# Mixture-of-experts kernel on one Trainium2 core: gathered rows scaled on the ScalarE and plainly transposed, routing by 8 one-hot products of nine columns

## Chip, core and metric

The kernel runs as one program on one core of a Trainium2 chip. The metric is the device time of one execution in microseconds (us); lower is better. The engines are named as the profile names them: PE (TensorE, matmuls), PEld (its weight loads), DVE (VectorE), ACT (ScalarE), POOL (GpSimd) and SP (SyncE, here the queue that issues the weight loads from memory).

## What is computed

One layer of a diffusion backbone over 1024 latent tokens of width 1024: a token mixer (differential attention and a short convolution), then an expert-choice mixture of experts with 16 experts of 128 token slots each. The change lies in the mixture of experts:

```python
logits = jnp.einsum('btd,de->bte', x_tok, w_router)
aff = jax.nn.softmax(logits, axis=-1)
g, idx = lax.top_k(jnp.swapaxes(aff, 1, 2), cap)      # cap = 128
xs = jax.vmap(lambda xt, ix: xt[ix])(x_tok, idx)
hg = jnp.einsum('becd,edf->becf', xs, w_gate)
hu = jnp.einsum('becd,edf->becf', xs, w_up)
y = jnp.einsum('becf,efd->becd', jax.nn.silu(hg) * hu, w_down) * g[..., None]
out = zeros.at[idx].add(y)
```

where `x_tok` is the normalised and modulated stream: each token's row times its reciprocal root mean square (one number per token), then a scale and a shift per channel.

## The kernel before

The mixer takes the first part of the span. From about 717 us on a loop runs over the 16 experts, called e0 to e15 here. An expert has 6 chunks of weights, and a chunk has 4 tiles q0 to q3 of 128 x 1024 f32 numbers (`raw`, 512 KB), which the SP queue loads ahead into 30 buffers. Chunks c0 and c2 are the two halves of the gate projection (products into `hg`), c1 and c3 those of the up-projection (`hu`), c4 and c5 the down-projection (`pyy`, two banks).

Every f32 product is made from three reduced ones. `split` (lines 155 to 159) divides a tile: ACT writes the rounded upper part `whi` (L157), then DVE the rest `wlo` (L158). There are 4 buffers of each (`NSP`), so the upper part of a tile can be written once PE is through with the tile four before. `mm3` then issues L162, L163 and L164: upper by upper, `wlo` by upper, `whi` by the lower part of the other operand. A tile takes 6 matmuls, a chunk 24, an expert 144.

For each expert `route` finds its tokens: DVE compares positions into a one-hot tile `oh` (L1460), 24 small products of 3 columns (L1465) sum token number (three parts), gate and token scale into the bank `pi`, ACT turns the first column into the index `idx` (L1467), POOL gathers the 128 rows `xs` from memory (L1469), DVE copies the three sums to `slot` (L1472) and builds `dgx`, the identity times the token scale (L1474). `xsplit` then transposes and scales at once, as eight f32 matmuls of `xs` blocks with `dgx` (L1511) into two banks `ptt`; ACT applies scale and shift per channel (`xsy`, L1513, eight instructions) and `split` gives `xsh` and `xsl`.

The loop body in code order: c0 products; the routing of the next expert (`nxt = route(e + 1)`); c1 products, `glu`; c2 products; transposes of the first activation half (`tsplit`, four, L1481, giving `ach` and `acl`); c3 products, `glu`; `xsplit` of the next expert; c4 and c5 with the transposes of the second half after the first tile (`TSJ`); then ACT scales the result by the gate (`y`, L1604) and POOL adds the rows into memory (`ffS`, L1605). e15 is different: its last chunks aren't split.

The code order isn't the queue order. SP's queue is written by hand; those of PE, DVE, ACT and POOL are laid out in this part by the framework when the program is built, by its own estimate of when operands are ready, and each engine then runs its own queue strictly in that order. So a change in one instruction can move others.

Of the kernel before, what the change touches and what calls it, by code (L numbers as in the profile page):

```python
# [10 lines left out]
F32 = mybir.dt.float32  # L11
# [3 lines left out]
AF = mybir.ActivationFunctionType  # L15
OP = mybir.AluOpType
AX = mybir.AxisListType
# [3 lines left out]
P = 128  # L21
# [5 lines left out]
E = 16  # L27
KT = 8
# [119 lines left out]
def build(tc, nc, I, out, dbg=None):  # L148
    V, S, G, PE, SY = nc.vector, nc.scalar, nc.gpsimd, nc.tensor, nc.sync
# [17 lines left out]
    with es:  # L167
# [4 lines left out]
        sm = es.enter_context(tc.tile_pool(name="sm", bufs=4))  # L172
        dr = es.enter_context(tc.tile_pool(name="dr", bufs=1, space=DRAM))
        pgA = es.enter_context(tc.tile_pool(name="pgA", bufs=NPA))
# [5 lines left out]
        def page(p, name, dt=F32, shape=(P, D)):  # L180
            return p.tile(list(shape), dt, name=name, tag="pg")

        def bank(shape, name):
            return psB.tile(list(shape), F32, name=name, tag="b")
# [219 lines left out]
        for i, o in enumerate(ORDER.split()):  # L404
            if i == NL0:
                npm = const("npm", [P, KT])
                ident = const("ident", [P, P])
# [100 lines left out]
        for i in range(10):  # L508
# [6 lines left out]
            for j in range(2):  # L515
                S.dma_start(out=vS[:, :, j, i, :].rearrange("h p e -> p h e"),
                            in_=f(hl[:, j, :]).rearrange("p (h e) -> p h e", h=H))
# [727 lines left out]
        for i, (h, qt) in enumerate(seq):  # L1245
            j = i + 2
# [26 lines left out]
            c = None  # L1273
            if SO[i // 16] == 0:
                if j < N:
                    c = score()
                x0 = transp(cs[i], qt, 0)
                x1 = transp(cs[i], qt, 1)
# [179 lines left out]
        def route(e):  # L1458
            oh = x1.tile([P, KT, P], BF, name="oh")
            V.tensor_tensor(out=oh, in0=late["iota"][:, None, :].to_broadcast([P, KT, P]),  # L1460
                            in1=pos[:, :, e:e + 1].to_broadcast([P, KT, P]), op=OP.is_equal)
            pi = bank([P, 3], "pi")
            for j in range(KT):
                for k in range(3):
                    PE.matmul(pi, oh[:, j, :], tokb[:, j, e, k, :], start=(j + k == 0), stop=(j == KT - 1 and k == 2))  # L1465
            idx = sm.tile([P, 1], I32, name="idx")
            S.activation(idx, pi[:, 0:1], AF.Copy)  # L1467
            xs = x1.tile([P, D], F32, name="xs")
            G.indirect_dma_start(out=xs, out_offset=None, in_=hS[:, :],  # L1469
                                 in_offset=bass.IndirectOffsetOnAxis(ap=idx[:, :1], axis=0))  # L1470
            s = sm.tile([P, 3], F32, name="slot")
            V.tensor_copy(out=s, in_=pi)  # L1472
            dg = x1.tile([P, P], F32, name="dgx")
            V.tensor_scalar(dg, ident, s[:, 2:3], None, op0=OP.mult)  # L1474
            g = s[:, 1:2]
            return idx, g, xs, s, dg

        def tsplit(src, k0, hi, lo):
            pp = bank([P, 4, P], "ptt")
# [21 lines left out]
                hi, lo = w[kt // 2]  # L1501
                mm3(ps, xh_[:, kt, :], xl_[:, kt, :], hi[:, kt % 2, :], lo[:, kt % 2, :], kt == 0, kt == KT - 1)

        def xsplit(xs, dg, eng=V):

            hi, lo = x1.tile([P, KT, P], F32R, name="xsh"), x1.tile([P, KT, P], F32R, name="xsl")
            for k in range(0, KT, 4):
                pp = bank([P, 4, P], "ptt")
                y = x1.tile([P, 4, P], F32, name="xsy", bufs=2)
                for j in range(4):  # L1510
                    PE.matmul(pp[:, j, :], xs[:, (k + j) * P:(k + j + 1) * P], dg, start=True, stop=True)  # L1511
                for j in range(4):
                    S.activation(y[:, j, :], pp[:, j, :], AF.Identity, bias=mv[:, 1, k + j:k + j + 1],  # L1513
                                 scale=mv[:, 2, k + j:k + j + 1])
                split(hi[:, k:k + 4, :], lo[:, k:k + 4, :], y, eng)
            return hi, lo
# [27 lines left out]

        cur = route(0)
        first = chunk(0, 0)
        xh_, xl_ = xsplit(cur[2], cur[4], V)
        eD.close()
        e5.close()
        for e in range(E):  # L1550
# [23 lines left out]
                prod(hu, xh_, xl_, chunk(e, 2 * fh + 1))  # L1574
                acts.append(glu(hg, hu))
            if e + 1 < E:
                xh_, xl_ = xsplit(nxt[2], nxt[4])
            pys = [eacc("pyy") for _ in range(2)]
            if e + 1 == E:

# [53 lines left out]
```

## Time and profile before

| | us |
|---|---|
| Median of 3 runs (1338.62 to 1341.94) | 1339.59 |
| The profiled execution's own time | 1337.48 |
| Its span in the profile | 1335.7 |
| PE busy | 1233.5 (92%) |
| DVE busy | 1076.9 (81%) |
| ACT busy | 794.9 (60%) |
| POOL busy | 67.9 (5%) |

Shares are means over the whole span. In the expert loop they differ: the slices from 780 us to 1180 us show PE at 9 tenths or more, DVE and ACT at 8 to 9, and the granted PE clock at full speed.

### The profile page before, as it was taken

To read this page: it belongs to the slowest core of one execution; us is meant where nothing else is said; L and a number is where in the kernel's file an instruction comes from. 1 tells how busy PE (TensorE), PEld (TensorE's weight loads), DVE (VectorE), ACT (ScalarE), POOL (GpSimd) and SP (SyncE) were. 2 spreads that over 40 slices of the span, in tenths; PEclk is the share of its full clock that TensorE was granted. 3 is DMA by queue.
4 is the path that set the end of the run, shared out by engine and by line. 5 is a ranking of instruction groups with operands and counts; after the bars stand their busy time and mean duration, and the time that the engine had idled before them with its cause. 6 is when DMAs were issued, how large, how long until landed. Compare 5 with 4: busy or idle time off the path is not lost. (4 is left out here: it accounts for less than half of the span.)

```text
span 1335.7 us, 18448 instructions
## 1 busy us (share of the span) xinstructions
PE 1233.5 (92%) x6407; PEld 1005.1 (75%) x6407; DVE 1076.9 (81%) x1834; ACT 794.9 (60%) x1183; POOL 67.9 (5%) x64
## 2 busy tenths in 40 slices
PE   6999999999999799989945999999999999999993
PEld 2587887888888578767844888888888888877761
DVE  5972565979698867798967999999999999888865
ACT  5731112434344544455443988888888888887861
POOL 0000000000000000000000000000000000010022
PEclk8999999999999899999956999999999999999997
DMA  9449448455466974333297999999999999999497
GB/s 350 140 81 319 148 148 252 135 166 182 134 179 183 297 192 143 129 120 124 107 407 244 320 393 370 384 381 380 372 378 373 377 377 371 379 356 363 120 377 161
DMA packets 139053, 347.69 MB, mean 260 GB/s; under 512 B 16976, under 2 KB 59472, under 8 KB 138320
## 3 DMA queue, kind: packets, MB, share of 16 engines
q1 hardware_dynamic: 109760, 306.14, 64.7%
q0 software_dynamic: 7056, 25.69, 7.3%
q10 hardware_dynamic: 22144, 14.68, 3.9%
q8 instruction: 50, 0.82, 0.2%
q14 instruction: 43, 0.35, 0.1%
HBM read 297.17 MB, written 49.30 MB: 259 GB/s over the span
## 5 line engine op out<-in xcount | busy, mean ns | idle before, releaser
L158 DVE TENSOR_TENSOR wlo<-raw,whi 128x1024 fp32r<-128x1024 f32 x376 | 440.8, 1220 | 33.1 <-ACT whi L157 27.9
L157 ACT ACTIVATE whi<-raw 128x1024 fp32r<-128x1024 f32 x376 | 388.7, 1066 | 61.7 <-PE hu L164 28.3
L1131 ACT ACTIVATE e<-ps,nm 128x1280 f32<-128x1280 f32 x64 | 84.4, 1327 | 65.5 <-DVE nm L1127 65.3
L1127 DVE TENSOR_REDUCE nm<-ps 128x1 f32<-128x1280 f32 x64 | 92.8, 1484 | 14.5 <-PE ps L1118 14.3
L162 PE MATMUL hu<-whi,xsh 128*128 128x512 f32 x256 | 102.7, 401 | 1.6 <-ACT whi L157 1.6
L163 PE MATMUL hu<-wlo,xsh 128*128 128x512 f32 x256 | 101.8, 398 | 0.8 <-DVE wlo L158 0.8
L164 PE MATMUL hg<-whi,xsl 128*128 128x512 f32 x256 | 99.8, 390 | 1.0 <-DVE xsl L158 1.0
L163 PE MATMUL hg<-wlo,xsh 128*128 128x512 f32 x256 | 100.4, 392 | 0.0
L164 PE MATMUL hu<-whi,xsl 128*128 128x512 f32 x256 | 100.4, 392 | 0.0
L162 PE MATMUL hg<-whi,xsh 128*128 128x512 f32 x256 | 100.0, 391 | 0.0
L1118 PE MATMUL ps<-KK,q 128*128 128x512 f32 (+1 forms) x384 | 90.8, 383 | 8.8 <-ACT e L1131 6.5
L1163 ACT ACTIVATE ath<-ptr 128x512 fp32r<-128x512 f32 (+1 forms) x96 | 47.8, 525 | 85.5 <-PE ptr L1158 85.1
L163 PE MATMUL pyy<-wlo,ach 128*128 128x512 f32 x240 | 95.0, 396 | 1.4 <-DVE wlo L158 0.9
L162 PE MATMUL pyy<-whi,ach 128*128 128x512 f32 x240 | 94.0, 402 | 0.0
L164 PE MATMUL pyy<-whi,acl 128*128 128x512 f32 x240 | 93.8, 391 | 0.0
L1118 PEld LDWEIGHTS ps<-KK,q 128*128 128x128 f32 x384 | 65.2, 202 | 20.9 <-ACT e L1131 9.1
L671 PE MATMUL pf<-xh,wh 128*128 128x512 f32 x192 | 75.1, 391 | 0.9 <-DVE gc L689 0.9
L675 PE MATMUL pf<-xh,wl 128*128 128x512 f32 x192 | 75.8, 395 | 0.0
L673 PE MATMUL pf<-xl,wh 128*128 128x512 f32 x192 | 75.2, 392 | 0.0
L1166 DVE TENSOR_TENSOR atl<-ptr,ath 128x512 fp32r<-128x512 f32 (+1 forms) x96 | 55.5, 596 | 14.3 <-ACT ath L1163 14.1
L162 PEld LDWEIGHTS hu<-whi,xsh 128*128 128x128 f32 x256 | 48.3, 189 | 11.4 <-ACT whi L157 2.1
L163 PEld LDWEIGHTS hu<-wlo,xsh 128*128 128x128 f32 x256 | 48.5, 190 | 11.1 <-DVE wlo L158 1.8
(316 smaller groups left out, 2649.1 us busy)
## 6 DMA issues: line engine op xcount, KB each, us to landing
raw<-in_we SPq DMA_DIRECT2D x384, 512.0 KB, 9.4
wa<-in_wa SPq DMA_DIRECT2D x32, 512.0 KB, 7.5
wraw<-in_wF SPq DMA_DIRECT2D x20, 512.0 KB, 5.2
waw<-in_wa SPq DMA_DIRECT2D x16, 512.0 KB, 6.9
q<-qS SPq DMA_DIRECT2D x64, 128.0 KB, 4.4
mS<-hl SPq DMA_DIRECT2D x48, 128.0 KB, 5.3
vS<-hv ACTq DMA_DIRECT2D x20, 256.0 KB, 6.0
KK<-kS SPq DMA_DIRECT2D x16, 320.0 KB, 8.5
```

What stands on the lines that cost most here:

```text
L157: i = S.activation(hi, src, AF.Copy)
L158: eng.tensor_sub(lo, src, f(hi))
L162: PE.matmul(ps, wh, mh, start=first, stop=False)
L163: PE.matmul(ps, wh, ml, start=False, stop=False)
L164: PE.matmul(ps, wl, mh, start=False, stop=last)
L671: PE.matmul(ps, wh[:, kt, :], xh[kt][:, sl], start=first, stop=False)
L673: PE.matmul(ps, wh[:, kt, :], xl[kt][:, sl], start=False, stop=False)
L675: PE.matmul(ps, wl[:, kt, :], xh[kt][:, sl], start=False, stop=last)
L1118: PE.matmul(ps[:, m, k0:k0 + n], q[:, m, j, :], KK[:, m, k0:k0 + n], start=(j == 0), stop=(j == 1))
L1127: V.tensor_reduce(out=c[1][-1], in_=c[0][:, m, :], axis=AX.X, op=OP.max, negate=True)
L1131: S.activation(e, c[0][:, m, :], AF.Exp, bias=c[1][3 + m], accum_out=l[:, m:m + 1])
L1166: V.tensor_sub(x[1], x[2], f(x[0]))
```

## The change

The eight products with `dgx` become plain transposes with the identity. The token scale is applied before them, by one ACT instruction over the gathered rows (in place; for e15 into a page of its own, because the unscaled rows are added at the end). For all but e0 this instruction must queue behind the last `whi` of chunk c3. The 24 products of 3 columns become 8 of 9 columns, and DVE sums the three parts (`tensor_reduce`) and makes the index (`tensor_copy`).

```diff
-            pi = bank([P, 3], "pi")
+            pi = bank([P, 9], "pi")
             for j in range(KT):
-                for k in range(3):
-                    PE.matmul(pi, oh[:, j, :], tokb[:, j, e, k, :], start=(j + k == 0), stop=(j == KT - 1 and k == 2))
+                PE.matmul(pi, oh[:, j, :], tokb[:, j, e, :, :].rearrange("p k c -> p (k c)"), start=(j == 0),
+                          stop=(j == KT - 1))
+            s = sm.tile([P, 3], F32, name="slot")
+            V.tensor_reduce(out=s, in_=pi.rearrange("p (k c) -> p c k", c=3), axis=AX.X, op=OP.add)
             idx = sm.tile([P, 1], I32, name="idx")
-            S.activation(idx, pi[:, 0:1], AF.Copy)
+            V.tensor_copy(out=idx, in_=s[:, 0:1])
             xs = x1.tile([P, D], F32, name="xs")
             G.indirect_dma_start(out=xs, out_offset=None, in_=hS[:, :],
                                  in_offset=bass.IndirectOffsetOnAxis(ap=idx[:, :1], axis=0))
-            s = sm.tile([P, 3], F32, name="slot")
-            V.tensor_copy(out=s, in_=pi)
-            dg = x1.tile([P, P], F32, name="dgx")
-            V.tensor_scalar(dg, ident, s[:, 2:3], None, op0=OP.mult)
-            g = s[:, 1:2]
-            return idx, g, xs, s, dg
+
+            xn = xs if e + 1 < E else page(pgA, "xn")
+            return idx, s[:, 1:2], xs, s, xn
...
-        def xsplit(xs, dg, eng=V):
+        def xsplit(cur, eng=V, behind=None):
 
             hi, lo = x1.tile([P, KT, P], F32R, name="xsh"), x1.tile([P, KT, P], F32R, name="xsl")
+            xs = cur[4]
+            if behind is None:
+                S.activation(xs, cur[2], AF.Copy, scale=cur[3][:, 2:3])
+            else:
+                with tc.issue_after(behind.ins):
+                    S.activation(xs, cur[2], AF.Copy, scale=cur[3][:, 2:3])
             for k in range(0, KT, 4):
                 pp = bank([P, 4, P], "ptt")
                 y = x1.tile([P, 4, P], F32, name="xsy", bufs=2)
                 for j in range(4):
-                    PE.matmul(pp[:, j, :], xs[:, (k + j) * P:(k + j + 1) * P], dg, start=True, stop=True)
+                    PE.transpose(out=pp[:, j, :], in_=xs[:, (k + j) * P:(k + j + 1) * P], identity=ident)
...
-        xh_, xl_ = xsplit(cur[2], cur[4], V)
+        xh_, xl_ = xsplit(cur, V)
...
             if e + 1 < E:
-                xh_, xl_ = xsplit(nxt[2], nxt[4])
+                xh_, xl_ = xsplit(nxt, behind=lasts[0])
```

The queues come out differently at three places. First ACT in e1 to e8, around the end of c2, before:

```order
L157 ACTIVATE whi<-raw 128x1024 x5
L1467 ACTIVATE idx<-pi 128x1
L1541 ACTIVATE act<-hg 128x512
L157 ACTIVATE whi<-raw 128x1024 x8
L157 ACTIVATE ach<-ptt 128x512
L1541 ACTIVATE act<-hg 128x512
L157 ACTIVATE whi<-raw 128x1024 x4
L1513 ACTIVATE xsy<-ptt,mv 128x128 x5
```

and with the change:

```order
L157 ACTIVATE whi<-raw 128x1024 x5
L1546 ACTIVATE act<-hg 128x512
L157 ACTIVATE whi<-raw 128x1024 x8
L157 ACTIVATE ach<-ptt 128x512
L1546 ACTIVATE act<-hg 128x512
L1511 ACTIVATE xs<-xs,slot 128x1024
L157 ACTIVATE whi<-raw 128x1024 x4
L1518 ACTIVATE xsy<-ptt,mv 128x128 x5
```

The index has gone, and the scale of `xs` stands ahead of the four splits of c4. On PE the `pi` products have moved at the same time from between c0 and c1 of an expert to inside the down-projection of the expert before (in e0 to e8 behind two matmuls of c5's first tile, in e9 to e13 behind c4's second tile).

Second, ACT in e10, from the end of c2 to the end of the transposed rows, with the change:

```order
L1546 ACTIVATE act<-hg 128x512
L157 ACTIVATE ach<-ptt 128x512
L157 ACTIVATE whi<-raw 128x1024 x2
L1511 ACTIVATE xs<-xs,slot 128x1024
L157 ACTIVATE whi<-raw 128x1024 x2
L1518 ACTIVATE xsy<-ptt,mv 128x128 x5
L157 ACTIVATE xsh<-xsy 128x512
L1518 ACTIVATE xsy<-ptt,mv 128x128 x3
L157 ACTIVATE whi<-raw 128x1024
L157 ACTIVATE xsh<-xsy 128x512
L157 ACTIVATE whi<-raw 128x1024
L157 ACTIVATE ach<-ptt 128x512
```

Here only c4's q0 and q1 are split ahead of the `xsy` instructions; q2 and q3 stand behind them. This layout holds in e9 to e13; before the change its like stands in e12 to e14 only. In e14 of the changed kernel all four tiles of c4 stand behind the `xsy` instructions.

Third, DVE in e10 from the end of c3 on, before:

```order
L1542 TENSOR_TENSOR act<-act,hu 128x512
L158 TENSOR_TENSOR wlo<-raw,whi 128x1024
L158 TENSOR_TENSOR xsl<-xsy,xsh 128x512
L158 TENSOR_TENSOR acl<-ptt,ach 128x512
L158 TENSOR_TENSOR xsl<-xsy,xsh 128x512
L158 TENSOR_TENSOR wlo<-raw,whi 128x1024 x11
L1460 TENSOR_TENSOR oh<-iota,pos 128x1024
```

and with the change:

```order
L1547 TENSOR_TENSOR act<-act,hu 128x512
L158 TENSOR_TENSOR wlo<-raw,whi 128x1024
L158 TENSOR_TENSOR xsl<-xsy,xsh 128x512
L1467 TENSOR_REDUCE slot<-pi 128x3
L1460 TENSOR_TENSOR oh<-iota,pos 128x1024
L158 TENSOR_TENSOR xsl<-xsy,xsh 128x512
L158 TENSOR_TENSOR wlo<-raw,whi 128x1024 x2
L158 TENSOR_TENSOR acl<-ptt,ach 128x512
L158 TENSOR_TENSOR wlo<-raw,whi 128x1024 x7
L1469 CAST idx<-slot 128x1
```

The sum of the routing products and the next one-hot tile now stand ahead of the second `xsl` and of the `wlo` of c4's q2 and q3.

## Rows read from the trace of the kernel before

**Rows 1.** Windows: us; busy us (xinstructions) of PE, PEld, DVE, ACT, POOL; clock; DMA; GB/s.

```profile
1086.00:1122.00 36.00, 36.00 (x193) 29.91 (x193) 32.96 (x34) 31.44 (x42) 3.22 (x2) 1.00 1.01 375
```

**Rows 2.** Timeline of PE in e2 (start us, us, engine line op, count).

```profile
802.45 0.76 PE L1465 MATMUL pi<-tokb,oh 128*128 128x3 bf16 x24
803.07 0.48 PE L162 MATMUL hu<-whi,xsh 128*128 128x512 f32 x1
...
820.02 1.95 PE L1511 MATMUL ptt<-dgx,xs 128*128 128x128 f32 x16
821.72 0.48 PE L162 MATMUL pyy<-whi,ach 128*128 128x512 f32 x1
...
827.95 0.41 PE L163 MATMUL pyy<-wlo,ach 128*128 128x512 f32 x1
...
833.21 0.39 PE L162 MATMUL hg<-whi,xsh 128*128 128x512 f32 x1
```

**Rows 3.** Timeline of ACT in the same expert.

```profile
816.20 1.06 ACT L157 ACTIVATE whi<-raw 128x1024 fp32r<-128x1024 f32 x1
...
820.21 1.06 ACT L157 ACTIVATE whi<-raw 128x1024 fp32r<-128x1024 f32 x1 [0.29 <-PE hu L164]
821.18 1.84 ACT L1513 ACTIVATE xsy<-ptt,mv 128x128 f32<-128x128 f32 x5
...
825.45 4.93 ACT L157 ACTIVATE whi<-raw 128x1024 fp32r<-128x1024 f32 x5
```

**Rows 4.** Timeline of DVE in the same expert.

```profile
826.57 8.04 DVE L158 TENSOR_TENSOR wlo<-raw,whi 128x1024 fp32r<-128x1024 f32 x7 [0.18 <-ACT whi L157]
835.24 1.23 DVE L158 TENSOR_TENSOR wlo<-raw,whi 128x1024 fp32r<-128x1024 f32 x1 [0.63 <-ACT whi L157]
```

**Rows 5.** Waits of PEld, 760 to 1158 us: total us, times, longest.

```profile
PEld pyy L163 <- DVE wlo L158: 1.7, 10, 0.2
```

**Rows 6.** Instructions on tile ptt: count, duration ns min/median/max, first and last start.

```profile
L1511 PE MATMUL ptt<-dgx,xs x256: 270/275/551, 719.3 to 1259.1; 128*128 128x128 f32 x128
...
L1481 PE MATMUL ptt<-ident,act x120: 270/272/276, 741.7 to 1261.1; 128*128 128x128 f32 x120
```

**Rows 7.** Timeline of DVE and PE at the start of the expert loop.

```profile
713.54 1.23 DVE L1460 TENSOR_TENSOR oh<-iota,pos 128x1024 bf16<-128x1024 f32 x1 [0.90 <-PE pi L1465]
...
719.34 0.55 PE L1511 MATMUL ptt<-dgx,xs 128*128 128x128 f32 x1 [5.83 <-DMA xs<-hS,idx]
```

**Rows 8.** Timeline of PE: first products of e9, e13, e14, e15, and two places in e12.

```profile
1050.13 0.39 PE L162 MATMUL hg<-whi,xsh 128*128 128x512 f32 x1
...
1181.80 1.39 PE L1511 MATMUL ptt<-dgx,xs 128*128 128x128 f32 x11
...
1191.81 0.50 PE L163 MATMUL pyy<-wlo,ach 128*128 128x512 f32 x1
...
1196.97 0.39 PE L162 MATMUL hg<-whi,xsh 128*128 128x512 f32 x1
...
1234.65 0.39 PE L162 MATMUL hg<-whi,xsh 128*128 128x512 f32 x1
...
1272.14 0.39 PE L162 MATMUL hg<-whi,xsh 128*128 128x512 f32 x1
```

**Rows 9.** Timeline of ACT in e12, behind the end of c3.

```profile
1182.66 1.85 ACT L1513 ACTIVATE xsy<-ptt,mv 128x128 f32<-128x128 f32 x5 [2.00 <-PE ptt L1511]
...
1185.94 1.09 ACT L157 ACTIVATE whi<-raw 128x1024 fp32r<-128x1024 f32 x1
1186.89 0.66 ACT L157 ACTIVATE xsh<-xsy 128x512 fp32r<-128x512 f32 x1
```

**Rows 10.** Windows, as rows 1: the loop's start, and the first up-projection of e15.

```profile
719.00:723.00 4.00, 3.66 (x19) 3.63 (x20) 0.70 (x1) 1.55 (x5) 0.00 (x0) 0.50 0.97 303
...
1281.00:1283.50 2.50, 2.50 (x6) 2.02 (x7) 2.50 (x3) 1.51 (x2) 0.00 (x0) 0.50 1.02 357
```

**Rows 11.** Landing times of the DMAs on tile idx.

```profile
DMA to landing us min/median/max: 3.4/8.7/10.5
```

## Prediction

> **What bounds the kernel now.** I read the page's slices first, then the windows of the expert loop, then the timelines of PE, ACT and DVE through one expert, then the list of waits, and last the end and the start of the loop. In the slices of the expert loop PE stands at 9 tenths or more, and in a stretch of one expert it is busy 36.00 of 36.00 us, with DVE at 32.96 and ACT at 31.44 [rows 1]. So a microsecond taken from PE's list is worth a microsecond, but only where the operands of the next matmul are there in time. The reader should see one place where they barely are. Behind the end of c3 (820.02) ACT splits c4's q3, which it could not do earlier because it waits for PE to free a buffer, then runs the eight `xsy` and three other steps, and only at 825.45 starts on c5 [rows 3]. DVE gets c5's first `wlo` done from 826.57 on [rows 4], and PE uses it at 827.95 [rows 2]. PE waits for such a `wlo` in the down-projection 10 times between 760 and 1158 us, 0.2 us at most [rows 5]. In other words ACT and DVE need 7.93 us from the end of c3 to c5's first tile, and PE's own work in between fills just that time.
>
> **The change, part by part.** The sum is made against the profiled execution, 1337.48 us; the median of the runs shown, 1339.59, is 2.11 above it. Times called "after c3" count from the end of c3 of the expert.
>
> *Transposes.* The 256 records of the old products for 16 experts are 16 passes per expert; the plain transposes of the activations have 120 records for 15 experts of eight, so one pass each [rows 6]. Eight passes instead of 16 take 0.85 us instead of 1.70 [rows 2]. In e1 to e8 this saves nothing. The ACT chain above starts at the end of c3 and has the same instructions as before, so c5's first `wlo` still comes 7.93 us after c3. PE merely waits there for what it saved. Term: 0.
>
> *Scale of the rows on ACT.* It is an instruction of the size of a split, about 1.06 us, or 0.97 in the queue [rows 3]. It stands ahead of c4's splits. q0 then moves from 816.20 to about 817.2, q1 to 818.2, q2 to 819.1, and q3 waits for PE until 820.21 in any case [rows 3]. The cover is the waiting ahead of these splits; if it were gone, up to 0.97 us would come onto the chain in every expert, 14 in all. Term: 0; the rows give no reason for more.
>
> *Routing products.* 24 products take 0.62 us between c0 and c1 [rows 2]. They leave that place altogether, and 8 of them, about 0.2 us, go into the wait at c5. The eight experts e1 to e8 save 0.62 each (e0 had its products ahead of the loop): -5.0. What is bought there must not run into DVE: the sum over three parts and the next one-hot, 1.23 us [rows 7], now come ahead of the eighth `wlo` at 835.24, which had waited 0.63 [rows 4]. It moves to about 835.9 and ends at 837.1, and PE needs it at 833.21 plus 19 matmuls of 0.23, at 837.5. So it fits, with 0.4 us to spare. The sum itself has no row of its own; it lies between 0 and the 1.23 of the one-hot, and I take 0.2, as the 0.15 to 0.3 us of DVE's other small tiles would have it.
>
> *e9 to e13: another layout of the queues.* Here ACT splits c4's q2 and q3 only behind the `xsy`. The kernel before has that in e12, where hg of the next expert starts 15.17 us after c3 (1196.97 less 1181.80, [rows 8]) against 13.19 in e2 (833.21 less 820.02, [rows 2]). In the changed queue DVE must also wait for `pi` and write the one-hot before the second `xsl`. `pi` ends on PE at 0.85 + 1.4 + 0.35 + 1.4 + 0.2 = 4.2 us after c3, so the sum starts near 4.5, the one-hot near 4.7, and the second `xsl` near 5.8, just when `xsh` (1186.89 plus 0.66, 5.75 after c3) is there [rows 9]. Behind it stand q2 (6.4 to 7.6), q3, `acl`, and from 9.2 on c5. PE gets c5's first `wlo` at about 10.5, against 10.01 in e12 (1191.81) [rows 8], and the next expert starts 15.7 after c3. The rest of an expert is 36.15 - 13.19 - 0.62 = 22.34 us (36.15 is the mean of the six from 833.21 to 1050.13, [rows 2, 8]). So an expert takes 38.0 us; five take 190.2. Before they took 1234.65 - 1050.13 = 184.5 [rows 8]. Term: +5.7, between +3 (if DVE's insertion is hidden) and +8.
>
> *e14.* All four tiles of c4 stand behind the `xsy`. With e12's steps the first is split 3.9 us after c3 and its `wlo` starts at 5.0; second `xsl`, three more `wlo` at 1.15 each and `acl` follow, c5's first comes at 12.1, and e15 starts 17.2 after c3. With 22.8 us for the front part (its chunks are interrupted by transposes) the expert takes 40.0, before 1272.14 - 1234.65 = 37.5 [rows 8]. Term: +2.5, between 0 and +4. e15 has the same queue but for one swap, which the end of its first chunk covers: 0.
>
> *PE's clock.* Where PE stands nearly empty the granted clock can fall: behind the wait at the start of e15's up-projection it was 0.50, that is 1.2 instead of 2.4 GHz, and six matmuls took 2.5 us [rows 10], 0.42 each instead of 0.23. That is 1.1 us lost in the stretch of this row; with what lies around it I take 1.4 for a fall. In e14 PE will be nearly empty from 1.4 to 6.1 us after c3, so I count one. In e9 to e13 the gap is 0.7 and then 2.1 us with two matmuls between, which may or may not do it; I count one of five. Term: +2.8, between 0 and +8.4.
>
> *Start of the loop.* The first gather is late by one one-hot (now queued ahead of the index on DVE, 1.14 in the queue), less 0.4 for the shorter `pi`, plus 0.2 for the sum. The rows landed at 719.34 [rows 7]; now they land near 720.3 and are scaled by 721.4. Eight passes instead of 16 at the clock of 0.50 granted there [rows 10] give back most of it, and the third matmul waits for DVE anyway. I take +1.0, between +0.2 and +1.9.
>
> The Trainium skill's page "TensorE: Matmul & The Clock Gate", section "Part 4: PE-mode transpose", says that transpose mode does not count as PE work for the clock gate in the usual way. By that rule the first products of e0 would start at half clock and the sum would be 1.4 us higher; no row here shows transposes with little else around them, so the sum goes without it.
>
> Sum: +1.0 - 5.0 + 5.7 + 2.5 + 2.8 = **+7.0 us**: 1344.5 for the profiled execution, 1346.6 against the median.
>
> **Rivals.** A: *the late layout costs nothing over the early one* (faster). Then e9 to e13 run at 35.53 like e1 to e8 (-6.9 instead of +5.7), e14 ends 1.9 earlier instead of 2.5 later, and no clock falls: +1.0 - 5.0 - 6.9 - 1.9 = -12.8, 1326.8 us. It decides at c4's q2: if its `wlo` is done by 5 us after c3, A holds. For it: DVE's `wlo` step of 1.15 is shorter than PE's 1.4 per tile, so it catches up. Against: e12 has this layout already and needs 2 us more [rows 8].
>
> B: *transposes do count, and PE is not emptied enough for the clock* (no change). Then e0 to e8 gain some 0.5 us more each, because ACT reaches `xsy` sooner, and no fall occurs: 7.0 - 4.5 - 2.8 = -0.3, 1339.3 us. For it: the transposes are ready earlier. Against: ACT starts `xsy` at 821.18 straight behind its split, without any wait for PE [rows 3].
>
> C: *the gather comes late* (much slower). The new gather follows the scatter of the expert before on POOL's queue, and its index comes on DVE behind the eighth `wlo`, at 837.1. It lands in 8.7 us in the median, 10.5 at most [rows 11], so at 846 to 848; the scale wants it one period after 816.2, at 851.7. If two transfers so close together need 5 us more, ACT stands with all splits behind it. Each further microsecond costs 14: 1360 us and more. Against: 4 to 6 us of margin.
>
> D, that the change doesn't do what it says, I give nothing: the queues show eight products and eight transposes.
>
> **How the numbers follow.** A difference of 0.3% (4.0 us) is about what a measurement of this kernel can tell from no change. The forecast has 0.55, A 0.12, B 0.25, C 0.08. The forecast itself, with its terms at their likelier bounds, spans +4 to +13, 1343 to 1353; nearly all of it is slower by over 0.3%, and I move 0.03 of it to no change. So slower 0.60, no change 0.28, faster 0.12. The range takes in the forecast, B with 3 us below it, and the lower end of C's neighbourhood: 1336 to 1355. It leaves out A and C, 0.20 together.
>
> **What would show it.** In the changed profile: no `pi` between c0 and c1, and c5's first L163 still 7.9 us after c3 in e1 to e8, with PE waiting about 0.5 us for DVE's `wlo` there; a period of 35.5 us in those and of 38 in e9 to e13, with a wait of about 2 us on the `wlo` of c4's q2; about 40 us for e14, with the clock at 0.50 for some microseconds behind it. If c5 is reached earlier than 7.5 us after c3 in e1 to e8, the zero for the transposes was wrong. If ACT waits for a DMA ahead of the scale, C was right. If e9 to e13 take under 37 us, the largest positive term was wrong, and with it the sign.

## The result, and the profile after

The changed kernel takes 1352.43 us (1346.24 to 1355.32) where the kernel before takes 1340.74 in the runs beside it: a ratio of 1.0082, interval 1.0062 to 1.0102. It is slower by 0.8%, 11 us. The profiled execution after took 1354.15 us, its span 1352.4. PE is busy for 1225.1 us instead of 1233.5: the change did take work from PE, and the time grew.

The table follows PE from the first `pi`. Each expert counts from its first `hg` to the next one's. A clock term is what the prediction put down for falls of PE's granted clock to its half level.

| Stretch (us) | before | after | difference | predicted |
|---|---|---|---|---|
| first `pi` to e0 | 10.94 | 14.86 | +3.9 | +1.0 |
| e0 | 37.24 | 36.98 | -0.3 | 0 |
| e1 to e8 | 289.26 | 282.62 | -6.6 | -5.0 |
| e9 to e13 | 184.51 | 194.14 | +9.6 | +5.7, clock +1.4 |
| e14 | 37.49 | 41.36 | +3.9 | +2.5, clock +1.4 |
| e15 to the end | 63.55 | 61.76 | -1.8 | 0 |
| sum | 623.0 | 631.7 | +8.7 | +7.0 |

Ahead of the first `pi` the profile after is 7.9 us longer (720.64 against 712.70), in code that is the same. In the experiments that point lies between 706.9 and 715.4, in e3 and e9, which have the change's code there, at 706.9 and 713.2. So nothing here shows it to be part of the change, whose own +8.7 us stand within the interval of the ratio (8.3 to 13.7 us).

Timeline of PE in e1 of the kernel after, from the end of c3 to the next expert:

```profile
794.74 1.04 PE L1516 MATMUL ptt<-ident,xs 128*128 128x128 f32 x8
...
802.02 0.36 PE L1464 MATMUL pi<-tokb,oh 128*128 128x9 bf16 x8
802.58 0.50 PE L163 MATMUL pyy<-wlo,ach 128*128 128x512 f32 x1 [0.20 <-DVE wlo L158]
...
807.74 0.39 PE L162 MATMUL hg<-whi,xsh 128*128 128x512 f32 x1
```

These answer to [rows 2]. The transposes are eight, `pi` stands ahead of c5's first product on a `wlo`, and that product comes 7.84 us after c3, as before (7.93), now with a wait of DVE in front of it. The waits of PE's loads in the same layout (760 to 1060 us) and in the late one (1055 to 1270), the counterparts of [rows 5]:

```profile
PEld pyy L163 <- DVE wlo L158: 3.2, 9, 0.4
...
PEld pyy L163 <- DVE wlo L158: 11.4, 9, 2.2
PEld hu L163 <- DVE wlo L158: 4.0, 7, 0.8
```

In the late layout the loads wait for a `wlo` in c3 (`hu`) as well. In e9 the down-projection looks different. First PE, then DVE:

```profile
1077.61 1.03 PE L1516 MATMUL ptt<-ident,xs 128*128 128x128 f32 x8
...
1081.71 0.36 PE L1464 MATMUL pi<-tokb,oh 128*128 128x9 bf16 x8
1082.66 0.73 PE L162 MATMUL pyy<-whi,ach 128*128 128x512 f32 x2 [0.60 <-ACT whi L157]
1085.20 0.50 PE L163 MATMUL pyy<-wlo,ach 128*128 128x512 f32 x1 [1.80 <-DVE wlo L158]
...
1088.07 0.50 PE L163 MATMUL pyy<-wlo,ach 128*128 128x512 f32 x1
...
1093.23 0.39 PE L162 MATMUL hg<-whi,xsh 128*128 128x512 f32 x1
```

```profile
1080.65 0.69 DVE L158 TENSOR_TENSOR xsl<-xsy,xsh 128x512 fp32r<-128x512 f32 x1 [1.02 <-ACT xsh L157]
1082.11 0.17 DVE L1467 TENSOR_REDUCE slot<-pi 128x3 f32<-128x9 f32 x1 [0.76 <-PE pi L1464]
1082.19 1.22 DVE L1460 TENSOR_TENSOR oh<-iota,pos 128x1024 bf16<-128x1024 f32 x1
1083.32 0.69 DVE L158 TENSOR_TENSOR xsl<-xsy,xsh 128x512 fp32r<-128x512 f32 x1
1083.92 2.36 DVE L158 TENSOR_TENSOR wlo<-raw,whi 128x1024 fp32r<-128x1024 f32 x2
```

PE has q0 and q1 of c4, then stands for the split of q2 (0.60) and for its `wlo` (1.80). DVE has waited for `pi`, written the one-hot and the second `xsl` before it can write that `wlo`. c5's first `wlo` is used 10.46 us after c3 and the next expert starts at 15.62.

In e11 to e13 a smaller loss comes ahead of that, in c3: from an expert's start to the end of its c3 they take 23.0 us, e9 and e10 22.5, e1 to e8 22.25. ACT and PE in e11:

```profile
1149.74 0.60 ACT L157 ACTIVATE ach<-ptt 128x512 fp32r<-128x512 f32 x1 [2.10 <-PE ptt L1480]
...
1153.09 0.50 PE L163 MATMUL hu<-wlo,xsh 128*128 128x512 f32 x1 [0.40 <-DVE wlo L158]
```

ACT stands for the transposes that `ach` reads, with c3's last two splits behind it, and PE later waits for the `wlo` of one of them. In e13 DVE has no further one-hot tile to write, as there is no e16, and the `wlo` of q2 stands ahead of the second `xsl`: e13 takes 37.89 us where e11, with the same 23.0 to the end of c3, takes 38.55.

In e14 PE stands longest, with all of c4 behind the `xsy`:

```profile
1272.70 0.82 PE L1516 MATMUL ptt<-ident,xn 128*128 128x128 f32 x6
...
1277.54 0.81 PE L162 MATMUL pyy<-whi,ach 128*128 128x512 f32 x2 [3.24 <-ACT whi L157]
1278.79 0.80 PE L163 MATMUL pyy<-wlo,ach 128*128 128x512 f32 x1 [0.44 <-DVE wlo L158]
```

Windows (columns as in [rows 1]): the full stretch of [rows 1], then the stretches behind the waits of e10, e12 and e14:

```profile
1086.00:1122.00 36.00, 34.94 (x166) 27.93 (x164) 30.76 (x32) 30.25 (x39) 3.62 (x2) 1.00 0.99 361
1124.40:1127.50 3.10, 3.10 (x9) 2.42 (x8) 3.10 (x5) 1.66 (x3) 0.00 (x0) 0.51 0.90 311
1202.90:1206.00 3.10, 3.10 (x9) 2.39 (x8) 3.10 (x5) 1.60 (x3) 0.00 (x0) 0.51 0.90 301
1278.00:1281.00 3.00, 2.56 (x7) 1.82 (x6) 3.00 (x4) 3.00 (x5) 0.00 (x0) 0.51 0.37 112
```

PE was busy for all of the 36.00 us before, now for 34.94. Behind three of these waits the granted clock was at its half level (0.51 as the mean of the window). e10 takes 39.55 us where e9 takes 38.13, and e12 40.02 where e11 takes 38.55: 1.4 and 1.5 us for a fall.

The start of the loop, DVE, POOL, ACT and PE in order, the counterpart of [rows 7]:

```profile
721.06 0.17 DVE L1467 TENSOR_REDUCE slot<-pi 128x3 f32<-128x9 f32 x1 [0.47 <-PE pi L1464]
721.14 1.22 DVE L1460 TENSOR_TENSOR oh<-iota,pos 128x1024 bf16<-128x1024 f32 x1
722.27 0.15 DVE L1469 CAST idx<-slot 128x1 int32<-128x1 f32 x1
...
723.38 1.22 POOL L1471 DMA_INDIRECT xs<-hS,idx  x1 [25.65 <-DVE idx L1469]
...
730.72 1.15 ACT L1508 ACTIVATE xs<-xs,slot 128x1024 f32<-128x1024 f32 x1 [31.67 <-DMA xs<-hS,idx]
...
731.92 1.97 PE L1516 MATMUL ptt<-ident,xs 128*128 128x128 f32 x8 [10.90 <-ACT xs L1508]
...
735.50 0.80 PE L162 MATMUL hg<-whi,xsh 128*128 128x512 f32 x1 [1.42 <-ACT xsh L157]
```

The gather is issued 2.74 us after the first `pi` (before: 714.01 less 712.70, 1.31) and its rows are there 7.3 us later (before 5.3).

### The profile page after: what moved, and what is told of

Read it like the earlier page. It is cut to its first block, busy times and chain, and to the rows that moved or that the text cites. A ratio compares the mean times of both kernels' runs of the same rounds, so it can differ in the third digit from the quotient of the medians.

```text
span 1352.4 us, 17676 instructions
## 1 busy us (share of the span) xinstructions
PE 1225.1 (91%) x6023; PEld 991.1 (73%) x6023; DVE 1072.9 (79%) x1834; ACT 806.8 (60%) x1183; POOL 118.3 (9%) x64
## 5 line engine op out<-in xcount | busy, mean ns | idle before, releaser
L163 PE MATMUL pyy<-wlo,ach 128*128 128x512 f32 x240 | 97.4, 406 | 10.6 <-DVE wlo L158 10.5
L1118 PE MATMUL ps<-KK,q 128*128 128x512 f32 (+1 forms) x384 | 93.8, 393 | 11.2 <-ACT e L1131 5.6
L1471 POOL DMA_INDIRECT xs<-hS,idx x16 | 73.7, 4604 | 77.1 <-DVE idx L1469 25.7
L163 PEld LDWEIGHTS pyy<-wlo,ach 128*128 128x128 f32 x240 | 46.4, 193 | 24.0 <-DVE wlo L158 15.6
```

Of the source, the lines that this page charges most:

```text
L163: PE.matmul(ps, wh, ml, start=False, stop=False)
L1118: PE.matmul(ps[:, m, k0:k0 + n], q[:, m, j, :], KK[:, m, k0:k0 + n], start=(j == 0), stop=(j == 1))
```

## The experiments

The theory to test: the loss is the late layout of ACT's and DVE's queues in e9 to e14 and the start of the loop; the parts of the change cost little in themselves. Rivals: the products in their new form, the scale on ACT, the gather behind the scatter. All kernels in one table (periods from PE's first products; ratio to the kernel before with interval):

| Kernel | ratio | start | e1-e8 | e9-e13 | e14 |
|---|---|---|---|---|---|
| before | 1 | 10.9 | 36.16 | 36.90 | 37.49 |
| the change | 1.0082 [1.0062, 1.0102] | 14.9 | 35.33 | 38.83 | 41.36 |
| e1 products alone | 0.9986 [0.9965, 1.0006] | 14.5 | 35.76 | 37.10 | 37.20 |
| e2 scale and transposes alone | 1.0065 [1.0040, 1.0090] | 11.4 | 35.23 | 39.52 | 42.33 |
| e3 change, ACT's order | 1.0057 [1.0036, 1.0078] | 14.9 | 35.23 | 39.52 | 36.52 |
| e9 change, DVE's order | 1.0015 [0.9994, 1.0035] | 14.1 | 35.22 | 37.88 | 42.62 |
| e4 change, both orders | 0.9918 [0.9890, 0.9947] | 13.7 | 35.22 | 36.49 | 36.49 |
| e5 the full early layout | 0.9851 [0.9831, 0.9871] | 12.1 | 35.22 | 35.24 | 35.28 |
| e6 e5, first index on ACT | 0.9847 [0.9827, 0.9867] | 11.8 | 35.21 | 35.24 | 35.23 |
| e7 before, early layout | 0.9977 [0.9960, 0.9994] | 11.0 | 36.17 | 36.73 | 35.97 |
| e8 e5, two scales | 0.9994 [0.9973, 1.0016] | 12.0 | 36.03 | 36.74 | 37.81 |
| e10 e6, `xsy` ahead of c4 | 1.0051 [1.0030, 1.0071] | 13.7 | 36.85 | 37.00 | 36.90 |
| e11 e5, no scale | 0.9976 [0.9957, 0.9995] | 13.5 | 35.22 | 38.32 | 35.71 |
| e12 e10, scale later | 0.9962 [0.9941, 0.9984] | 13.3 | 35.95 | 36.27 | 36.90 |

**The two halves, e1 and e2.** e1 takes the lines of `route`, e2 those of `xsplit`, each into the kernel before. The core of e1 is `pi` with nine columns and

```diff
-            S.activation(idx, pi[:, 0:1], AF.Copy)
+            V.tensor_reduce(out=s, in_=pi.rearrange("p (k c) -> p c k", c=3), axis=AX.X, op=OP.add)
+            V.tensor_copy(out=idx, in_=s[:, 0:1])
```

> The kernel before with the routing products alone changed: eight products of nine columns, the sum of three parts and the index on DVE; the scaled diagonal and the 16 passes of the old transposes stay. Its queues keep the early layout (all splits of c4 ahead of the xsy) up to about e10, and pi stays between c0 and c1. Theory 'layout' (the change loses by the order of ACT and DVE in e9 to e14, its parts cost little): 8 passes (0.2 us) instead of 24 (0.62) in e1 to e14 give -5.9 us at most, the start of the loop costs +1 to +4 because the first index comes later on DVE, mixed experts at the end 0 to +2; so 1334 to 1341 us where before has 1340.7, a ratio of 0.995 to 1.000. Rival 'products' (the new form of the products with its sum and index on DVE is what costs): most of the change's +11 us stands here too, 1346 us or more, and the experts e1 to e8 are longer than before's 36.15.

e2 has the scale and the transposes:

```diff
-                    PE.matmul(pp[:, j, :], xs[:, (k + j) * P:(k + j + 1) * P], dg, start=True, stop=True)
+                    PE.transpose(out=pp[:, j, :], in_=xs[:, (k + j) * P:(k + j + 1) * P], identity=ident)
```

> The kernel before with the scale on ACT and the plain transposes alone; 24 one-hot products of three columns and the index on ACT as before. Its queues have the late layout in e9 to e13 and e14 as the change has. Theory 'layout': e1 to e8 near 35.3 to 35.7 us (pi has moved behind c5 and lies in the wait there), e9 to e13 near 38 to 39 where before has 36.9, e14 near 41 where before has 37.5, start of the loop +1; together +5 to +9, 1346 to 1350 us. Rival 'products': no loss is left, 1340 us or less. Rival 'scale' (the scale of the rows on ACT itself costs, 1.15 us in each expert): e1 to e8 are longer than in the change, 36 us or more, and the time is 1350 us or more.

Both went as the layout theory has it: 1335.76 and 1346.69 us. The products alone bring 0.40 per expert in e1 to e8 (36.16 to 35.76) and cost 3.6 at the start. The other half has the late layout in e9 to e13 and the loss. Its late experts are slower than the change's by another 0.7, and than the 38 to 39 that was said: behind their waits the granted clock stood at 0.50 in e9, e10 and e11 (40.16 to 40.35 us each), in the change in two experts of the five. So the products are not what costs; they only cost at the start.

**The order undone: e3, e9, e4.** The instructions are the change's. e3 changes ACT's queue:

```diff
+                w4 = chunk(e, 4)
-                xh_, xl_ = xsplit(nxt, behind=lasts[0])
+                xh_, xl_ = xsplit(nxt, behind=last3, after=lasts[0])
...
+                with tc.issue_after(after.ins) if after is not None else ExitStack():
                     for j in range(4):
                         S.activation(y[:, j, :], pp[:, j, :], AF.Identity, bias=mv[:, 1, k + j:k + j + 1],
```

> The change with ACT's order forced into the early layout: the four splits of c4 stand ahead of the xsy in every expert, as in e1 to e8 already; DVE in e9 to e13 still has the sum of pi and the one-hot between the two xsl. Instructions are the same. Theory 'layout': e9 to e13 fall from 38.8 to 35.5 to 36.5 us each (-12 to -17 together), e14 from 41.4 to about 37 (-4), so 1332 to 1338 us. Rival 'scale' or 'gather' (the scale on ACT, or the gather behind the scatter on POOL, is what costs): the order changes little, 1348 us or more, and ACT waits for the gathered rows or PE for c4's first tile instead. The part on DVE is told from the part on ACT by the next run.

e9 changes DVE's (`lo` is the `wlo` of c0's q2, `casts[0]` the last index):

```diff
+            with behind_(casts[0]):
                 V.tensor_tensor(out=oh, in0=late["iota"][:, None, :].to_broadcast([P, KT, P]),
...
+            with behind_(lo):
                 V.tensor_reduce(out=s, in_=pi.rearrange("p (k c) -> p c k", c=3), axis=AX.X, op=OP.add)
```

> The change with DVE's order alone forced (sum of pi behind the next chunk's wlo, one-hot behind the index); ACT keeps the late layout in e9 to e13. With e3 (ACT's order alone) and e4 (both) this makes a square. Theory 'DVE' (the sum of pi and the one-hot between the two xsl are what costs, since DVE waits there for PE and PE then for DVE): e9 to e13 take what ACT's late layout costs by itself, 1.5 us over 35.2 as e13 had over its forced layout in the kernel before (37.67 against 36.12), so 36.7 to 37.3, e14 38 to 40; the time is 1335 to 1340 us, a ratio of 0.997 to 1.001, far under the change. Theory 'ACT' (the late splits of c4 are what costs): e9 to e13 stay at 38 to 39, 1348 us or more.

e4 has both edits.

> The change with ACT's order as in the run before and DVE's forced too: the sum of pi behind the wlo of the next chunk's third tile, the next one-hot behind the index of this one, in every expert. Instructions are the same. Theory 'layout': all of e1 to e14 take 35.3 us like e1 to e8 of the change, 14 x 35.3 = 494.2 where the change has 282.6 + 194.1 + 41.4 = 518.1; with the one-hot of the first expert out of the way another -1 at the start: 1327 to 1331 us, a ratio to before of 0.990 to 0.993. If DVE's order was no part of the loss, this is equal to the run before within 2 us. Rival 'scale' or 'gather': 1345 us or more.

e3 missed by far: 1344.48 us, and e9 to e13 were slower than in the change. Timeline of e3's e9, DVE and then PE, and a window behind it:

```profile
1068.42 0.69 DVE L158 TENSOR_TENSOR xsl<-xsy,xsh 128x512 fp32r<-128x512 f32 x1
1071.44 0.17 DVE L1467 TENSOR_REDUCE slot<-pi 128x3 f32<-128x9 f32 x1 [2.33 <-PE pi L1464]
1071.52 1.22 DVE L1460 TENSOR_TENSOR oh<-iota,pos 128x1024 bf16<-128x1024 f32 x1
...
1073.85 5.76 DVE L158 TENSOR_TENSOR wlo<-raw,whi 128x1024 fp32r<-128x1024 f32 x5
...
1071.04 0.36 PE L1464 MATMUL pi<-tokb,oh 128*128 128x9 bf16 x8
...
1075.12 0.50 PE L163 MATMUL pyy<-wlo,ach 128*128 128x512 f32 x1 [3.05 <-DVE wlo L158]
...
1075.80:1078.80 3.00, 3.00 (x9) 2.33 (x8) 3.00 (x4) 1.06 (x1) 0.00 (x0) 0.50 0.80 228
```

With c4 early PE reaches `pi` only after all of c4, DVE stands 2.33 us for it, and PE then stands 3.05 for the `wlo` that DVE has behind the sum, the one-hot, `xsl` and `acl`. Each waits for the other in turn. The clock fell behind that wait in e9, e10 and e11 (40.15 to 41.13 us); e12, where it did not, takes 38.53, as e11 of the change does (38.55). So ACT's order alone gains nothing in these experts: the wait moves from c4's q2 to c5, and what is slower than the change is time at the half clock. What e3 gains in all is e14's, 41.36 to 36.52.

e9, with ACT's late layout kept, took 1341.40 us where 1335 to 1340 was said, with 37.88 in e9 to e13 instead of 36.7 to 37.3 and 42.62 in e14 instead of 38 to 40. That layout alone costs 2.6 us over 35.24, and DVE's order of the change 0.66 more (e11 of the change, 38.55, against 37.88 here and 37.89 in e13 of the change), besides the falls of the clock (none in e9's e9 to e13). Neither order is the whole cause by itself: e9 to e13 take 194.1 us in the change, 197.6 in e3, 189.4 in e9 (2.9 of this gain are the two falls) and 182.4 in e4, with both.

e4 came out at the lower bound of what was said, 1327.09, but not in the way it was said, so the hit is luck: e9 to e14 kept 36.49. Timeline of ACT in e4's e9:

```profile
1061.09 0.60 ACT L159 ACTIVATE ach<-ptt 128x512 fp32r<-128x512 f32 x1 [2.12 <-PE ptt L1489]
```

**The rest of the order: e5.** In e4's late experts `ach` stands ahead of c3's last two splits, as in the change's, and ACT waits 2.12 us for its transposes with those two splits behind it.

```diff
+                    w3 = chunk(e, 3)
-                    tsplit(acts[0], 0, ach, acl)
+                    tsplit(acts[0], 0, ach, acl, behind=lasts[0])
...
+            with tc.issue_after(lasts[0].ins) if lasts[0] is not None else ExitStack():
                 lasts[1] = S.activation(a, hg, AF.Silu)
```

> The run e4 (both orders forced) still has 36.49 us in e9 to e14 against 35.2 in e1 to e8; there ACT takes the first transposed activations (ach) one split sooner and stands for PE (2.1 us in each expert), and DVE's last wlo of c3 and of c5's neighbour come 0.8 and 0.9 us late. Here the silu is queued behind the last split of its chunk and ach behind c3's last split, as e1 to e8 have it; ACT's queue is then the same in e1 to e14. Theory 'layout': e9 to e14 fall to 35.2 to 35.3 too, 6 x 1.27 = -7.6 us against e4: 1318 to 1321 us, a ratio to before of 0.984 to 0.987. Rival 'data' (these experts are slow by something that is no order: their weight loads, or the gather that follows the scatter): 36.5 stays, 1326 us or more.

Measured 1315.74 us. First products of e1 and e15 on PE in e5:

```profile
759.89 0.39 PE L164 MATMUL hg<-whi,xsh 128*128 128x512 f32 x1
...
1253.09 0.39 PE L164 MATMUL hg<-whi,xsh 128*128 128x512 f32 x1
```

Fourteen experts in 493.20 us are 35.23 each; the change took 518.1. So the 2.6 us of ACT's late layout are two things: 1.4 for c4's splits behind the `xsy` (37.88 to 36.49), 1.25 for the place of `ach` and the silu (36.49 to 35.24). The gather still follows the scatter on POOL in e4 and e5, and in e9 to e14 of the change the scale waits for the rows nowhere, so that rival has no part in what these experts lose. Between the change and e5 lies nothing but the order of the same instructions, and 2.3% (1.0082 over 0.9851).

**Is it the layout or the change? e7.** The same order on the kernel before; besides e5's two edits and the `after` of e3:

```diff
-                xh_, xl_ = xsplit(nxt[2], nxt[4])
+                w4 = chunk(e, 4)
+                xh_, xl_ = xsplit(nxt[2], nxt[4], after=lasts[0])
```

> The kernel before, its instructions unchanged, with the early layout forced in all experts (c4's splits ahead of the xsy, silu and ach behind their chunk's last split). Theory 'layout': the only experts that had another one, e12 to e14 (38.43, 37.67 and 37.49 us), fall to 36.14 as e1 to e11: -5.2 us, a ratio of 0.995 to 0.997. Then what the change itself is worth at equal layout is e5 against this run: 14 x (36.14 - 35.22) = -12.9, +3 at the start, about -10 us. Rival (the layout costs nothing in the kernel before; these experts are slow by something else): 1338 us, a ratio of 1.000.

1333.50 us, a ratio of 0.9977 where 0.995 to 0.997 was said. e13 and e14 fell as expected, to 36.12 and 35.97; e12 did not (39.07), since there PE's queue still came out mixed with the transposes. At nearly equal layout the change is worth 1.3% (0.9851 against 0.9977): 0.95 per expert in e1 to e8.

**The start: e6.**

```diff
+            if e:
                 casts[0] = V.tensor_copy(out=idx, in_=s[:, 0:1])
+            else:
+                S.activation(idx, s[:, 0:1], AF.Copy)
```

> The run e5 with the first expert's index written by ACT instead of DVE. Theory: of the change's +3.9 us between the first one-hot product and the first product of e0, 1.2 were the one-hot ahead of the index (gone since e4), about 0.7 the step from DVE to POOL (0.96 us from the end of the cast to the gather's issue, against 0.3 behind ACT), and the rest the weight loads, which start 0.2 us behind the gather instead of 2.3. So the gather is issued 0.5 to 0.8 us sooner, and e0 starts 0.7 to 1.5 us sooner after the first product than in e5 (13.7 in e4); -0.7 to -1.5 us. Rival: the landing is set by the loads alone: less than 0.3 us.

Too much was expected: 11.8 instead of 12.1 us, and no difference in the time. The step to POOL did shorten, from 0.96 to 0.30 us. But e4 and e5 have this stretch in the same order, and the rows landed 7.2 us after the issue in the one and 5.6 in the other. That difference is open.

**The price of the scale: e8 and e11.** e8 puts a plain copy of the rows ahead of the scale; e11 has none in e1 to e14.

```diff
+                    S.activation(xs, cur[2], AF.Copy)
                     S.activation(xs, cur[2], AF.Copy, scale=cur[3][:, 2:3])
```

> The run e5 with a plain copy of the gathered rows, of the same size, ahead of the scale on ACT: 1.15 us more of ACT's time in each expert, beside c4's splits. The result is the same. Theory 'the scale is hidden' (ACT waits for PE ahead of c4's third and fourth tile for longer than that): experts stay within 0.3 us of 35.2, the time within 4 us of e5. Rival 'scale': each expert gets 0.8 to 1.15 us longer, +11 to +16 us against e5, and by the same measure the scale itself costs the change as much.

> The run e5 without the scale on ACT in e1 to e14: the gathered rows are transposed unscaled, so this part of the computation is left out. Only e1 to e8, whose order stays as it was, are to be compared (from e10 on the order is another). With e5 (one scale) and e8 (two, 36.03 us) this gives the price of the first. Theory 'hidden': e1 to e8 stay at 35.2 us within 0.1, so that ACT's waiting ahead of c4's last tile covers one scale but not two. Rival 'scale': they fall by up to 0.8 us, to 34.6 (where PE's own work would be the bound), and the scale took that much of the change's gain.

e1 to e8 take 35.22 without a scale, 35.22 with one, 36.03 with two. (From e12 on e8 fell back to the late layout, 37.8 each, so its 1335.92 us are more than the price of a scale.) Timeline of ACT in e8's, e5's and e11's e2:

```profile
820.21 1.06 ACT L1523 ACTIVATE xs<-xs 128x1024 f32<-128x1024 f32 x1
821.16 2.00 ACT L159 ACTIVATE whi<-raw 128x1024 fp32r<-128x1024 f32 x2
823.05 1.14 ACT L1524 ACTIVATE xs<-xs,slot 128x1024 f32<-128x1024 f32 x1
824.10 1.04 ACT L159 ACTIVATE whi<-raw 128x1024 fp32r<-128x1024 f32 x1
...
815.57 3.07 ACT L159 ACTIVATE whi<-raw 128x1024 fp32r<-128x1024 f32 x3
...
814.37 1.06 ACT L159 ACTIVATE whi<-raw 128x1024 fp32r<-128x1024 f32 x1 [0.21 <-PE hu L166]
815.73 1.06 ACT L159 ACTIVATE whi<-raw 128x1024 fp32r<-128x1024 f32 x1 [0.30 <-PE hu L166]
817.09 1.06 ACT L159 ACTIVATE whi<-raw 128x1024 fp32r<-128x1024 f32 x1 [0.30 <-PE hu L166]
```

With two scales ACT works without a gap. With one it just does so too (e5), with none it waits for PE three times ahead of these splits, 0.8 us in all (e11). So one scale fills the waiting that was named as its cover, and of a second 0.81 us comes onto the path of every expert. In e11 the late layout came back from e10 on, though there is no scale: ACT's extra instruction is not what turns the order.

**Further than e5: e10 and e12.** The eight `xsy` ahead of c4's splits, to shorten the chain behind c3:

```diff
+                    nx = xsplit(nxt, behind=l2, after=lasts[0])
...
+                xh_, xl_ = xfin(nx, after=lasts[0])
```

> A version that goes on from e6: the next expert's scale stands behind c2's splits, its eight transposes are traced ahead of c3's products and the eight xsy behind c3's last split, so that after the end of c3 ACT has only xsh, ach and c5 to do. In e6 PE has some 0.5 us without work in each expert, at c5's first wlo. Theory (the chain on ACT from the end of c3 to c5 is what bounds the expert at 35.2 us): the wait goes, e1 to e11 take 34.6 to 34.9 us, -4 to -8 us against e6 in all: 1308 to 1313 us, a ratio to before near 0.980. Rival (DVE, busy for some 33 us of each expert, is the bound with its own waits, or the scale no longer finds cover there): 35.2 or more.

It missed, 1345.94 us. Timeline of ACT in e10's e3:

```profile
848.93 1.15 ACT L1526 ACTIVATE xs<-xs,slot 128x1024 f32<-128x1024 f32 x1 [1.80 <-DMA xs<-hS,idx]
```

The gathered rows were not there yet, and all splits stood behind the scale: rival C of the prediction, a chunk earlier. e12 moves the scale by two splits:

```diff
-                    nx = xsplit(nxt, behind=l2, after=lasts[0])
+                    nx = xsplit(nxt, behind=lq[1], after=lasts[0])
```

> The run e10 with the scale two splits later in ACT's queue, behind the second split of c3. In e10 the scale stood 1.7 us for the gathered rows in each expert (the gather is issued 4.1 us after the start of an expert and takes 9.5 to 10.7 us to land, so 13.6 to 14.8; ACT was there at 12.1), and e1 to e11 took 36.9 us instead of the expected 34.8. Theory 'gather' (that wait alone made e10 slow): ACT is there at 14.8, does not wait, and the experts take 34.7 to 35.0 us: 1308 to 1313 us. Rival 'chain' (what stood ahead of c4's first split, eight xsy and a silu, is what cost, so that c4 comes late whenever the xsy stand there): 35.5 to 36.5 us, 1320 to 1333 us, with PE waiting for c4's first wlo.

1331.14 us, and 35.87 in most experts: 'chain'. Timeline of ACT in e12's e3, then PE at the first `wlo` of c4 (whose products start at 862.02) and of c5:

```profile
857.07 2.88 ACT L1536 ACTIVATE xsy<-ptt,mv 128x128 f32<-128x128 f32 x8
859.81 0.63 ACT L1572 ACTIVATE act<-hg 128x512 f32<-128x512 f32 x1
860.29 3.94 ACT L159 ACTIVATE whi<-raw 128x1024 fp32r<-128x1024 f32 x4
...
862.70 0.50 PE L165 MATMUL pyy<-wlo,ach 128*128 128x512 f32 x1
...
869.65 0.50 PE L165 MATMUL pyy<-wlo,ach 128*128 128x512 f32 x1 [0.53 <-DVE wlo L160]
```

The gather's wait cost about 1 us per expert (36.85 to 35.95). But even without it c4's splits start only at 860.29, behind the `xsy`, and c4's first `wlo` is used 0.7 us after c3's last product, in e5 0.3 behind its transposes. The eight transposes, now ahead of the end of c3, gain nothing by it: c5's first `wlo` comes 7.6 us after c3, where 7.84 less their 0.79 would be 7.05, and PE stands 0.53 us for it. Behind c3 the `xsy` had lain beside PE's work on c4; ahead of it they delay c4. The best versions stay e5 and e6.

## Why the prediction was right, step by step

The sign, the layout and its place were right, and the range held the result. That the sum is so near, +7.0 against +8.7, is in part luck: the start (+2.9) and e9 to e13 (+2.5) came out above their terms, e1 to e8 (-1.6) and e15 (-1.8) below. Step by step:

- *Transposes, 0 in e1 to e8*: right. c5's first product on a `wlo` comes 7.84 us after c3 where 7.93 was said (7.83 to 8.21 in the eight). PE waits there, 0.4 at most.
- *Scale on ACT, 0*: right and shown (e8, e11). The price given for a lost cover, up to 0.97 in each expert, is near the 0.81 of a second scale.
- *Routing products, -5.0*: -6.6. The eight products disappear in the wait at c5 as said, and PE gets a further 0.2 back per expert.
- *e9 to e13, +5.7*: the mechanism is right to a tenth of a microsecond in e9. The sum of `pi` was to start 4.5 us after c3 and did at 4.50; the second `xsl` near 5.8, at 5.71; c5 at 10.5, at 10.46; the next expert at 15.7, at 15.62. The expert takes 38.13 where 38.0 was said. The five take 2.5 more than the 5.7 and 1.4 that were said. Two falls of the clock came where one of five was counted, each of about the 1.4 that was named. And the rest of an expert was put at 22.34 us, as the early experts have it, where the place of `ach` and the silu makes it 22.5 in e9 and e10 and 23.0 in e11 to e13: +2.2. e13, taken for one like the others, has no one-hot on DVE and gives 0.8 of this back. Not foreseen either is that ACT's and DVE's orders hold each other: undoing ACT's alone (e3) gains nothing there.
- *e14, +2.5 and a fall of 1.4*: the mechanism is right, the exact sum luck. The first `wlo` was to come 6.1 us after c3 (5.0 plus its 1.15) and was used at 6.09; 41.36 us against 40.0 + 1.4. But up to the end of c3 it took 23.45 where 22.8 was said, and from there 17.91 where 17.2 + 1.4 was said.
- *Start, +1.0 within 0.2 to 1.9*: this step failed, with +3.9. Its first sentence left out two things. The step from DVE to POOL takes 0.96 us (722.42 to 723.38) where ACT's took 0.30, so the issue moved by 1.4 and not by 0.9. And the landing was taken as unchanged, 5.3 us, where it took 7.3; the loads start 0.2 us behind the gather instead of 2.3, but e5 has them as close and landed in 5.6, so that cause is not shown. In e0, behind the transposes, the first seven products also ran at the half level, 0.43 us each to 738.7; before, behind twice as many passes, the clock was up by the second. The Trainium skill's "TensorE: Matmul & The Clock Gate", section "Part 4: PE-mode transpose", says that transposes don't count for the clock as PE work does; by that rule the prediction named 1.4 us more. The rows agree with it, but do not show it: eight passes are half the work of before in any case, and PE then waited 1.42 us. And e0 as a whole still came out 0.3 us shorter.
- *e15, 0*: -1.8; why is open.

Of the rivals, A fell: the late layout costs 2.6 us per expert with DVE's order put right, 2.9 and more without. It decided at c4's q2 as said; its `wlo` was to be done by 5 us after c3 and was used at 7.59. B fell with three clock falls (e10, e12, e14) that the kernel before does not have. C came as far as its condition: in e1 to e9 the rows land 13.8 us after the gather's issue instead of 8.4 (the 8.7 of [rows 11] counts the scatters too), 5 us later as C has it, if not by the two transfers it named (last section). That used up the margin of 4 to 6 us: the scale waits for the rows in e2, e5 and e8, 0.38, 0.28 and 0.17 us, and these are the ones among e1 to e8 that take 35.37 to 35.58 us. e10 shows what more would cost.

## What to carry to other kernels

A change that takes work from the engine that bounds the loop can lose by the order in which the others' queues come out. Compare the order of every iteration, not of one: here eight iterations gained 0.8 us each and six lost 0.2 to 3.9. Where a scheduler decides the order, pin the order of the good iterations before judging an edit: the same instructions gave 1.008 and 0.985. And pin both engines of a loop of waits; with ACT alone in order, DVE and PE waited for each other, and nothing was gained in those experts.

## What the runs showed of the hardware that was not expected

The gather's instruction on POOL grew from 1.63 to 6.91 us in e1 to e9 of the change. Timeline of DVE, then POOL, in e2:

```profile
811.66 6.90 DVE L158 TENSOR_TENSOR wlo<-raw,whi 128x1024 fp32r<-128x1024 f32 x6
...
812.50 6.91 POOL L1471 DMA_INDIRECT xs<-hS,idx  x1 [1.69 <-PE hg L164]
```

It ends 0.85 us after the last of six `wlo` that follow each other without a gap, in all nine gathers from 777 to 1060 us, and the rows land after 13.8 us in the median instead of 8.4. The Trainium skill's "GPSIMD Engine Reference", section "1. Specifications", says that POOL shares its ways to SBUF with DVE and gets in conflict with DVE instructions that read two tiles there, as `wlo` does. The rows of the change agree; e4's do not, where the gather starts as deep in an unbroken run of `wlo` (801.71, DVE from 800.87) and takes 1.24 us. What makes the difference is open. It cost the change 0.8 us, the waits in e2, e5 and e8 told above; elsewhere the scale comes later than the rows.

The first gather follows the end of its index by 0.30 us where ACT wrote it (before, e6) and by 0.95 to 0.96 where DVE did (the change, e4).
